# Rows of w_ada loaded one weight chunk ahead of their dot products, with other rates, in a two-layer encoder kernel

## The chip, the cores and the metric

The kernel runs on one core of one Trainium2 chip. The metric is the device time of the whole program in microseconds (us), from runs of the program without a profiler; a trace of one profiled execution stands beside them. On the core, TensorE (PE, with its weight loads as PEld) multiplies matrices, VectorE (DVE), ScalarE (ACT) and GpSimd (POOL) work on elements, and SyncE (SP) issues most of the DMAs. Each engine executes its own instructions in a fixed order; semaphores hold an instruction back until what it reads is there and what it overwrites is no longer needed.

## What is computed

Input is x (512 tokens of 1024 channels) and one conditioning vector c. Two layers, each of three sub-layers on x, each after a norm that is modulated by c:

```python
# mod: for each layer 9 vectors of 1024: silu(c) @ w_ada + b_ada
# (shift, scale, gate) of FFN 1: j = 0, 1, 2; mixer: j = 3, 4, 5; FFN 2: j = 6, 7, 8
h = rms_norm(x, gain) * (1 + scale) + shift
x += 0.5 * gate * ((silu(h @ w_gate) * (h @ w_up)) @ w_down)              # FFN, d_ff = 2816
proj = h @ w_in                                                           # mixer
ya = chunked_relpos_attention(qa, ka, va, ...)
yb = multiscale_pool(ub, w_pool, pool_scale)
yc = forgetting_attention(qc, kc, vc, f, ...)
merged = sum(sigmoid(g_n) * (y_n @ w_branch[n]) for n in (a, b, c))
x += gate * (merged @ w_out)
# then a second FFN with its own shift, scale and gate
```

All is in 32-bit floats. c is known from the start, so the 2 x 9 vectors depend on nothing else that is computed: they have to be there when the norm (shift, scale) or the residual addition (gate) uses them.

## The kernel before

x and the activations lie transposed: 8 blocks of 128 channels, 512 tokens in the free dimension. Every 32-bit operand of a product is split into a high and a low part, and a product is three matmuls (hi·hi, lo·hi, hi·lo: the three lines L119, L120, L121, all in one helper).

**Weights.** `wchunk` (L262) brings a chunk of 512 KB: a DMA on SP's queue into `raw` (L266; 2 buffers), the high part by a cast on ACT into `whi` (L277), the low part by a subtraction on DVE into `wlo` (L279); `whi` and `wlo` have 3 buffers each. A matmul with `wlo` can't begin before that subtraction; the cast can't begin before PE has let go of the buffer. The first thing that `wchunk` does is `side_work`, below.

**Modulation vectors.** Each of the 2 x 9 vectors is 8 blocks of 128, so there are 144 pieces. A piece (`mod_step`, L200) is a DMA of the 128x1024 rows of w_ada (512 KB, on SP's queue, L203) and a dot product with silu(c) on DVE (L206, a multiply with a running sum and a short read of that sum), for a scale also L215 and for a gate L217, on 128x1. 16 of them are done while the program starts, with their own code. The other 128 wait in a queue, in the order layer, j, block, and are taken out by `side_work`: each weight chunk adds MOD_RATE to a credit, and for each whole credit one piece is taken, load and dot together, ahead of the chunk's own load. So on SP a w_ada load stands before a weight load, and on DVE the dot stands before that chunk's subtraction. `mod_need(l, j)` takes out whatever is still missing up to vector j of layer l, at once. It is asked before a norm and before a residual addition.

The rates: 1.0 in the first part of an FFN's gate and up products, 0 in its later parts (which run a 7-product scheme, `seven`), `(1.9, 1.2, 1.5, 1.2)[2 * l + s]` in the down products (FFN s of layer l), 1.0 in the merges of the mixer; none in the attention stages. The rows lie in buffers of the tag "v2" (4 buffers, shared with activations) in the FFNs and of the tag "b" (17 buffers) in the merges.

**Stages.** An FFN runs over d_ff in three parts (6, 8 and 8 blocks of 128 of the 22): gate and up products with the activation, then a down product for the two halves of the output channels (`k_outer`, a weight chunk of 2 blocks of d_ff times 512 channels each; the part of 6 blocks has 2 x 3 chunks). The residual additions are L434 on DVE. The third part takes nothing from the queue once the next sub-layer's norm has been prepared. The mixer does its projections, the attention of branch A and that of branch C with the merge of A between, and then, each as a run of units: four pooling pieces (`pool_front`, with additions on GpSimd, L1033), the merge of C and the merge of B (`merge_units`): for each of 8 blocks d a gate chunk (w_ubg, products with hhi and hlo) and, for every second d, a branch chunk (w_branch) for two d's, then the sum of their products on DVE (L1142) and POOL. After them comes the product with w_out. "Even gates" are those of even d, ahead of which a branch chunk stands.

The order of the work on each engine is that in which the program is written; a table of delayed steps (`later`, `poll`) interleaves the norms and the pooling with the products.

Of the kernel before, what the change touches and what calls it, by code (L numbers as in the profile page):

```python
# [40 lines left out]
def encoder_kernel(tc, xT, c, w_ada, b_ada, gains, w_gate, w_up, w_down, w_qkv, w_f, w_ubg,  # L41
# [22 lines left out]
    def st(shape, dt, tag, bufs):  # L64
        return sb.tile(shape, dt, tag=tag, bufs=bufs, name=nm(tag))
# [4 lines left out]
    def mmt(shape=(P, T)):  # L70
        return ps.tile(list(shape), F32, tag="mm", bufs=4, name=nm("mm"))
# [17 lines left out]
    class Task:  # L89
# [3 lines left out]
        def run(self):  # L93
            fn, self.fn = self.fn, None
            if fn is not None:
                fn()

    def later(delay, fn, group=None):
        t = Task(pe[0] + delay, fn, group)
        tasks.append(t)  # L100
        return t
# [85 lines left out]
    @contextlib.contextmanager  # L187
    def after(what):

        if what in last:  # L190
            with tc.issue_after(last[what]):
                yield
        else:
            yield
# [5 lines left out]
    def mod_step(l, j, d, tag="raw"):  # L200
        raw = st([P, D], F32, tag, {"v2": 4, "raw": NRAW, "b": NB}[tag])
        with after("dma"):
            nc.sync.dma_start(raw, w_ada[l, j, d])  # L203
        m = modc[:, l, j, d:d + 1]
        with after("norm"):
            dot = nc.vector.tensor_tensor_reduce(out=raw, in0=raw, in1=silc[0], scale=1.0,  # L206
                                                 scalar=badac[:, l, j, d:d + 1], op0=ALU.mult, op1=ALU.add,
                                                 accum_out=m).ins
        s, kind = divmod(j, 3)
        if kind == 1:  # L210
            g = gainc[:, l, s, d:d + 1]
            if in_start[0]:
                nc.scalar.activation(apre[:, l, s, d:d + 1], m, AF.Identity, scale=g, bias=g)
                return dot
            return nc.vector.scalar_tensor_tensor(apre[:, l, s, d:d + 1], m, 1.0, g, op0=ALU.add, op1=ALU.mult).ins  # L215
        if kind == 2:
            nc.vector.tensor_scalar(m, m, 0.5, None, op0=ALU.mult)  # L217

    mod_queue = [(l, j, d) for l in range(L) for j in range(9) for d in range(KD)][16:]
    mod_ptr = [0]  # L220
    in_start = [True]
    mod_credit = [0.0]

    mod_tag = ["v2"]

    def mod_pop():
        if mod_ptr[0] < len(mod_queue):
            mod_step(*mod_queue[mod_ptr[0]], mod_tag[0])
            mod_ptr[0] += 1

    def mod_need(l, j):
        while mod_ptr[0] < min(len(mod_queue), (l * 9 + j + 1) * 8 - 16):
            mod_pop()

    MOD_RATE = [1.0]
    in_ffn = [True]
# [12 lines left out]
            yield  # L249

    def side_work(side=True):
        if quiet[0] > 0:
            quiet[0] -= 1
            if quiet[0] == 0:
                gate.clear()
        elif side and in_ffn[0] and mod_tag[0] != "raw":
            mod_credit[0] += MOD_RATE[0]
            while mod_credit[0] >= 1.0:
                mod_credit[0] -= 1.0
                mod_pop()  # L260
# [41 lines left out]
    def xd(d):  # L302
        return x_blocks[d // 2][:, d % 2, :]
# [249 lines left out]
    def apply(parts, func, **kw):  # L553

        o = t1(T)
        n = T // len(parts)
        for i, p in enumerate(parts):
            nc.scalar.activation(o[:, i * n:(i + 1) * n], p, func, **kw)
        return o


    class Ffn:
# [7 lines left out]
        def prefetch(self, xtag):  # L570
            mod_need(self.l, 3 * self.ms + 1)
            self.norm = Norm(self.l, self.ms, xtag)
# [22 lines left out]
        def run(self, nxt):  # L595
            l, s, ms = self.l, self.s, self.ms
            in_ffn[0] = True
            mod_tag[0] = "v2"
            parts = ((0, 6), (6, 8), (14, 8))
            for part, (f0, nf) in enumerate(parts):  # L600
                acts = []
                n = 0
                if part == 0 and self.norm is None:
                    acts = self.start()
                    n = 3
                    blocks = Blocks()
                elif part == 0:
                    g0, u0, g1 = self.pre
                    pg, pu, pg1 = mmt(), mmt(), mmt()
                    for hs in range(2):  # L610
                        self.norm.back(hs, acc if hs else mmt)
                        cols = slice(hs * HALF, (hs + 1) * HALF)
                        if hs == 0:
                            later(FRONT1, lambda: self.norm.front(1, acc))
                            later(BACK1, lambda: self.norm.back(1, acc))
                        for k in range(KD):
                            self.unit(pg, g0, cols, (k,))
                            self.unit(pu, u0, cols, (k,))
                        self.unit(pg1, g1, cols)
                    u1 = self.gate_up(1, 1)  # L620
                    acts.append(self.act(0, pg, pu))
                    pu1 = mmt()
                    self.unit(pu1, u1)
                    acts.append(self.act(1, pg1, pu1))
                    n = 2
                    blocks = Blocks(self.norm.xa, modc[:, l, 3 * ms])
                if part == 0:
                    blocks.schedule(T_FIRST, T_STEP)
                elif part == 1:
                    blocks.finish()  # L630
                MOD_RATE[0] = 0.0 if part else 1.0
                while part and n < nf:
                    both = [apply(p, AF.Silu)
                            for p in seven([w_gate[l, s, f0 + n + i] for i in range(2)], blocks, acc)]
                    ups = seven([w_up[l, s, f0 + n + i] for i in range(2)], blocks, mmt)
                    for i, sg in enumerate(both):
                        acts.append(self.act(n + i, None, ups[i], sg))
                    n += 2
                while n < nf:
                    g = self.gate_up(0, f0 + n)  # L640
                    u = self.gate_up(1, f0 + n)
                    pg, pu = mmt(), mmt()
                    self.unit(pg, g)
                    self.unit(pu, u)
                    acts.append(self.act(n, pg, pu))
                    n += 1
                mod_need(l, 3 * ms + 2)
                MOD_RATE[0] = (1.9, 1.2, 1.5, 1.2)[2 * l + s]
                for c0 in (0, T):
                    def src(c):  # L650
                        r0 = (f0 + 2 * c) * P
                        return w_down[l, s, r0:r0 + 2 * P, c0:c0 + T].rearrange("(k p) c -> p k c", p=P)

                    def ops(hi, lo, kt, j):
                        return (hi[:, j * P:(j + 1) * P], lo[:, j * P:(j + 1) * P],
                                acts[kt][:, 0, :], acts[kt][:, 1, :])

                    last = part == len(parts) - 1
                    if last and c0 == 0 and nxt is not None:
                        nxt.prefetch("v2")  # L660
                        mod_tag[0] = "raw"
                    split = last and c0 > 0
                    hook = None
                    if split:
                        hook = nxt.prefetch_weights if nxt is not None else (lambda: None)
                    for j, hs, o in k_outer(src, nf // 2, ops, hook):
                        d = c0 // P + j
                        residual_tail(d, hs, o, modc[:, l, 3 * ms + 2, d:d + 1], nxt if last else None)
                        if last and nxt is None:
                            cols = slice(0, T) if hs is None else slice(hs * HALF, (hs + 1) * HALF)  # L670
                            nc.sync.dma_start(out[:, d, cols], xd(d)[:, cols])
# [420 lines left out]
    def drain(*gens):  # L1092
        for it in gens:
            for _ in it:
                pass

    class Mixer:
# [1 line left out]
            self.l = l  # L1099

        def prefetch(self, xtag):
            mod_need(self.l, 5)
            self.norm = Norm(self.l, 1, xtag)

        def prefetch_weights(self):
# [2 lines left out]
        def run(self, nxt):  # L1108
            l = self.l
# [56 lines left out]
            for gi in range(4):  # L1166
                b = pool_front(l, gi)
                later(60, lambda gi=gi, b=b: pool_back(l, gi, b, wp, yb))
            in_ffn[0], mod_tag[0], MOD_RATE[0] = True, "b", 1.0
            drain(mc)  # L1170
            poll(True)
            mb = merge_units(l, 1, yb, put_b)
# [8 lines left out]
            for c0 in (0, T):  # L1181
# [8 lines left out]
                for j, hs, o in k_outer(src, 4, ops, nxt.prefetch_weights if c0 else None):  # L1190
                    d = c0 // P + j
# [70 lines left out]
```

## Time and profile before

| | |
|---|---|
| median of 3 runs | 2403.73 us (2403.13 to 2406.02) |
| the profiled execution | 2404.73 us |
| its span, first to last instruction | 2403.0 us, clock 1.00 |
| PE busy | 2359.9 us, 98% |
| DVE busy | 1725.9 us, 72% |
| ACT busy | 1198.4 us, 50% |
| POOL busy | 351.7 us, 15% |
| loads of w_ada | 96 into "v2", 48 into "b", 512 KB each |

A row of a timeline gives start, duration (both us), engine, source line, operation, output <- input by the program's names, shape, and in brackets how long the engine had been idle before it and what it then waited for. Durations of matmuls overlap, since they are pipelined; their starts tell what one costs.

### The profile page before, as it was taken

How to read it: one execution, taken by the hardware profiler on the slowest of the kernel's cores; microseconds unless marked ns; L12 is line 12 of the kernel's file. 1: busy time of each engine (PE TensorE's matmuls, PEld its weight loads, DVE VectorE, ACT ScalarE, POOL GpSimd, SP SyncE). 2: the span in 40 equal slices, each digit the busy share in tenths (PEclk: the TensorE clock that was granted, in tenths of full speed). 3: DMA queues.
4: the chain of work that ended last, by engine and by line, in shares of the span. 5: the costliest groups of instructions: out<-in, count | busy, mean ns of one | idle time of the engine just before them, and what ended most of it. 6: DMA issues, size and time to landing. Idle time of an engine off the chain costs nothing. (4 is left out here: it accounts for less than half of the span.)

```text
span 2403.0 us, 36815 instructions
## 1 busy us (share of the span) xinstructions
PE 2359.9 (98%) x14106; PEld 2085.6 (87%) x14106; DVE 1725.9 (72%) x3070; ACT 1198.4 (50%) x2090; POOL 351.7 (15%) x423
## 2 busy tenths in 40 slices
PE   7999999999999999999999999999999999999999
PEld 5799998778878898989998989978787788989898
DVE  8988866787665476878677878577866655658583
ACT  5353555786632353535553626466865324536252
POOL 3000011144432210000100000102444322000000
PEclk9999999999999999999999999999999999999999
DMA  7736342323345424353325353423233554223322
GB/s 274 238 113 228 99 152 84 93 79 109 108 171 201 175 98 166 105 186 105 132 83 196 104 197 106 141 79 98 80 116 108 193 182 169 71 97 106 101 96 103
DMA packets 116438, 320.94 MB, mean 134 GB/s; under 512 B 11139, under 2 KB 13315, under 8 KB 116261
## 3 DMA queue, kind: packets, MB, share of 16 engines
q1 hardware_dynamic: 115106, 314.38, 38.7%
q0 software_dynamic: 1152, 4.19, 0.4%
q8 instruction: 111, 1.82, 0.3%
q14 instruction: 67, 0.54, 0.1%
q10 hardware_dynamic: 2, 0.00, 0.0%
HBM read 312.16 MB, written 6.38 MB: 133 GB/s over the span
## 5 line engine op out<-in xcount | busy, mean ns | idle before, releaser
L277 ACT CAST whi<-raw 128x1024 fp32r<-128x1024 f32 (+1 forms) x267 | 277.4, 1043 | 431.5 <-PE acc L120 217.9
L279 DVE TENSOR_TENSOR wlo<-raw,whi 128x1024 fp32r<-128x1024 f32 x259 | 319.4, 1237 | 162.2 <-ACT whi L277 159.0
L119 PE MATMUL acc<-b,whi 128*128 128x512 f32 (+1 forms) x960 | 360.7, 376 | 0.2 <-DVE xv L434 0.2
L121 PE MATMUL acc<-b,wlo 128*128 128x512 f32 (+1 forms) x960 | 356.7, 372 | 1.8 <-DVE wlo L279 1.8
L120 PE MATMUL acc<-b,whi 128*128 128x512 f32 (+1 forms) x960 | 357.1, 372 | 0.0
L121 PEld LDWEIGHTS acc<-b,wlo 128*128 128x128 f32 x960 | 180.8, 188 | 34.0 <-DVE wlo L279 2.6
L119 PEld LDWEIGHTS acc<-b,whi 128*128 128x128 f32 x960 | 180.8, 188 | 31.8 <-DVE xv L434 0.6
L120 PEld LDWEIGHTS acc<-b,whi 128*128 128x128 f32 x960 | 181.0, 189 | 29.8
L119 PE MATMUL acc<-hhi,whi 128*128 128x512 f32 x480 | 191.3, 400 | 6.8 <-DVE b L1051 3.1
L121 PE MATMUL acc<-hhi,wlo 128*128 128x512 f32 x480 | 188.1, 393 | 1.0 <-DVE wlo L279 1.0
L120 PE MATMUL acc<-hlo,whi 128*128 128x512 f32 x480 | 188.6, 393 | 0.2 <-DVE hlo L711 0.2
L384 ACT CAST ptb<-v 128x1024 fp32r<-128x1024 f32 x128 | 134.0, 1050 | 97.7 <-DVE v L452 56.2
L385 DVE TENSOR_TENSOR ptb<-v,ptb 128x1024 fp32r<-128x1024 f32 x128 | 156.3, 1223 | 33.8 <-ACT ptb L384 32.3
L384 ACT CAST whi<-raw 128x1024 fp32r<-128x1024 f32 (+1 forms) x128 | 106.7, 834 | 92.1 <-PE acc L120 41.9
L119 PE MATMUL acc<-whi,hhi 128*128 128x512 f32 x336 | 137.8, 411 | 0.9 <-DVE xv L385 0.9
L206 DVE CUSTOM_DVE_ANT_0 v<-v,b,badac 128x1024 f32<-128x1024 f32 x96 | 127.1, 1333 | 15.0 <-DMA v<-in_w_ada_dram 14.8
L121 PE MATMUL acc<-whi,hlo 128*128 128x512 f32 x336 | 131.9, 393 | 0.0
L120 PE MATMUL acc<-wlo,hhi 128*128 128x512 f32 x336 | 131.6, 392 | 0.0
L385 DVE TENSOR_TENSOR wlo<-raw,whi 128x1024 fp32r<-128x1024 f32 (+1 forms) x128 | 121.6, 950 | 6.5 <-ACT whi L384 5.0
L434 DVE SCALAR_TENSOR_TENSOR xv<-acc,modc,xv 128x512 f32<-128x512 f32 (+1 forms) x112 | 77.3, 690 | 62.2 <-PE acc L121 62.0
L119 PEld LDWEIGHTS acc<-hhi,whi 128*128 128x128 f32 x480 | 90.6, 189 | 25.6 <-DVE b L1051 4.0
L329 POOL TENSOR_TENSOR ssum<-ssum,t 128x256 f32<-128x256 f32 (+1 forms) x45 | 46.5, 1034 | 442.8 <-ACT t L328 442.7
(315 smaller groups left out, 6667.5 us busy)
## 6 DMA issues: line engine op xcount, KB each, us to landing
v<-in_w_ada_dram SPq DMA_DIRECT2D x96, 512.0 KB, 5.3
raw<-in_w_down_dram SPq DMA_DIRECT2D x88, 512.0 KB, 3.7
raw<-in_w_up_dram SPq DMA_DIRECT2D x82, 512.0 KB, 4.0
raw<-in_w_gate_dram SPq DMA_DIRECT2D x79, 512.0 KB, 3.7
raw<-in_w_ubg_dram SPq DMA_DIRECT2D x56, 512.0 KB, 3.6
b<-in_w_ada_dram SPq DMA_DIRECT2D x48, 512.0 KB, 4.6
raw<-in_w_qkv_dram SPq DMA_DIRECT2D x42, 512.0 KB, 3.9
raw<-in_w_branch_dram SPq DMA_DIRECT2D x24, 512.0 KB, 3.7
```

Of the source, the lines that this page charges most:

```text
L119: mm(o, lh, rh, start=start, stop=False)
L120: mm(o, lh, rl, start=False, stop=False)
L121: mm(o, ll, rh, start=False, stop=stop)
L206: dot = nc.vector.tensor_tensor_reduce(out=raw, in0=raw, in1=silc[0], scale=1.0, scalar=badac[:, l, j, d:d + 1], op0=ALU.mult, op1=ALU.add ...
L277: nc.scalar.copy(hi, raw)
L279: lo_eng.tensor_tensor(lo, raw, hi.bitcast(F32), op=ALU.subtract)
L329: nc.gpsimd.tensor_tensor(self.ssum[:, cols], self.ssum[:, cols], q, op=ALU.add)
L384: nc.scalar.copy(hi, src)
L385: nc.vector.tensor_tensor(lo, src, hi.bitcast(F32), op=ALU.subtract)
L434: nc.vector.scalar_tensor_tensor(x, acc_j, gate, x, op0=ALU.mult, op1=ALU.add)
```

## The change

Outside the start of the program, taking a piece from the queue now issues the load only. The dot is kept in a list, and is written out at the beginning of the next chunk's `side_work` (`mod_flush`), or when a further piece is taken out within the same chunk (then all but the last one kept are written out). `mod_need` keeps up to two loads ahead while it takes several, and writes out the dots up to what it was asked for. Beside that, the mixer's norm asks for vectors up to j = 4 in place of 5 (the gate of the mixer is asked for before the w_out product, as it was before), the rate in all down products is 1.2, and that in the merges 1.2.

```diff
@@ mod_step
         with after("dma"):
             nc.sync.dma_start(raw, w_ada[l, j, d])
+        dot = lambda: mod_dot(raw, l, j, d)
+        return dot() if in_start[0] else dot
+
+    def mod_dot(raw, l, j, d):
         m = modc[:, l, j, d:d + 1]
...
-    def mod_pop():
+    loaded = []
+
+    def mod_pop(behind=1):
+        mod_flush(behind)
         if mod_ptr[0] < len(mod_queue):
-            mod_step(*mod_queue[mod_ptr[0]], mod_tag[0])
+            loaded.append(mod_step(*mod_queue[mod_ptr[0]], mod_tag[0]))
             mod_ptr[0] += 1
 
+    def mod_due(l, j):
+        return min(len(mod_queue), (l * 9 + j + 1) * 8 - 16)
+
+    def mod_flush(behind=0):
+        while len(loaded) > behind:
+            loaded.pop(0)()
+
     def mod_need(l, j):
-        while mod_ptr[0] < min(len(mod_queue), (l * 9 + j + 1) * 8 - 16):
-            mod_pop()
+        while mod_ptr[0] < mod_due(l, j):
+            mod_pop(2)
+        while mod_ptr[0] - len(loaded) < mod_due(l, j):
+            loaded.pop(0)()
...
     def side_work(side=True):
+        mod_flush()
         if quiet[0] > 0:
...
-                MOD_RATE[0] = (1.9, 1.2, 1.5, 1.2)[2 * l + s]
+                MOD_RATE[0] = 1.2
...
-            mod_need(self.l, 5)
+            mod_need(self.l, 4)
...
-            in_ffn[0], mod_tag[0], MOD_RATE[0] = True, "b", 1.0
+            in_ffn[0], mod_tag[0], MOD_RATE[0] = True, "b", 1.2
```

The number of loads taken in each stage, counted on SP:

| stage | before | after |
|---|---|---|
| layer 0, FFN 1, first down product | 13 | 9 |
| layer 0, FFN 1, second down product | 15 | 9 |
| layer 0, merges and w_out | 24 | 29 |
| layer 0, FFN 2 | 21 | 21 |
| layer 1, FFN 1 | 25 | 23 |
| layer 1, merges and w_out | 24 | 28 |
| layer 1, FFN 2, first part | 0 | 3 |

The other 22 loads, the same number in both, are in the time before the first down product. Two places show the order. The first is VectorE at the end of layer 0's first down product; `wlo` are splits of weight chunks, L206 (L210 after) dots, L434 (L451) residual additions. Before:

```order
L434 SCALAR_TENSOR_TENSOR xv_85<-acc_756,modc,xv_85 128x512
L206 ISA v_180_923,modc<-v_180_923,b_73,badac 128x1024
L206 ISA modc 128x1
L279 TENSOR_TENSOR wlo_930<-raw_927,whi_929 128x1024
L215 SCALAR_TENSOR_TENSOR apre<-modc,gainc 128x1
L206 ISA v_184_933,modc<-v_184_933,b_73,badac 128x1024
L206 ISA modc 128x1
L206 ISA v_185_937,modc<-v_185_937,b_73,badac 128x1024
L206 ISA modc 128x1
L215 SCALAR_TENSOR_TENSOR apre<-modc,gainc 128x1
L279 TENSOR_TENSOR wlo_944<-raw_941,whi_943 128x1024
```

And after, at the same two splits:

```order
L210 ISA v_176_911,modc<-v_176_911,b_73,badac 128x1024
L210 ISA modc 128x1
L451 SCALAR_TENSOR_TENSOR xv_78<-acc_754,modc,xv_78 128x512
L210 ISA v_180_920,modc<-v_180_920,b_73,badac 128x1024
L210 ISA modc 128x1
L210 ISA v_181_922,modc<-v_181_922,b_73,badac 128x1024
L210 ISA modc 128x1
L451 SCALAR_TENSOR_TENSOR xv_85<-acc_755,modc,xv_85 128x512
L296 TENSOR_TENSOR wlo_916<-raw_913,whi_915 128x1024
L451 SCALAR_TENSOR_TENSOR xv_85<-acc_756,modc,xv_85 128x512
L296 TENSOR_TENSOR wlo_927<-raw_924,whi_926 128x1024
```

Between the last two splits stood two dots, and stands one residual addition.

The second place is layer 1's merge of branch C, from a branch chunk's split to that of the gate of d = 4. VectorE before:

```order
L279 TENSOR_TENSOR wlo_19713<-raw_19710,whi_19712 128x1024
L206 ISA b_19716,modc<-b_19716,b_19248,badac 128x1024
L206 ISA modc 128x1
L1142 SCALAR_TENSOR_TENSOR t_3695_19652<-t_3693_19637,acc_19639 128x512
L206 ISA b_19768,modc<-b_19768,b_19248,badac 128x1024
L206 ISA modc 128x1
L215 SCALAR_TENSOR_TENSOR apre<-modc,gainc 128x1
L206 ISA b_19821,modc<-b_19821,b_19248,badac 128x1024
L206 ISA modc 128x1
L279 TENSOR_TENSOR wlo_19722<-raw_19719,whi_19721 128x1024
```

VectorE after:

```order
L1159 SCALAR_TENSOR_TENSOR t_3689_19629<-t_3687_19614,acc_19616 128x512
L296 TENSOR_TENSOR wlo_19694<-raw_19691,whi_19693 128x1024
L210 ISA b_19698,modc<-b_19698,b_19220,badac 128x1024
L210 ISA modc 128x1
L210 ISA b_19750,modc<-b_19750,b_19220,badac 128x1024
L210 ISA modc 128x1
L296 TENSOR_TENSOR wlo_19703<-raw_19700,whi_19702 128x1024
```

Between the two splits stood three dots, and stand two. SyncE's issues there, before (`raw` from w_branch and w_ubg are weight chunks, `b` from w_ada rows):

```order
L266 DMA raw_19710<-in_w_branch_dram 128x2x512
L203 DMA b_19716<-in_w_ada_dram 128x1024
L266 DMA raw_19719<-in_w_ubg_dram 128x1024
L203 DMA b_19768<-in_w_ada_dram 128x1024
L266 DMA raw_19772<-in_w_ubg_dram 128x1024
L203 DMA b_19821<-in_w_ada_dram 128x1024
```

And after:

```order
L283 DMA raw_19691<-in_w_branch_dram 128x2x512
L203 DMA b_19698<-in_w_ada_dram 128x1024
L283 DMA raw_19700<-in_w_ubg_dram 128x1024
L203 DMA b_19750<-in_w_ada_dram 128x1024
L283 DMA raw_19752<-in_w_ubg_dram 128x1024
L203 DMA b_19802<-in_w_ada_dram 128x1024
```

The last row of w_ada that stands ahead of the gate's split (b_19821 before, b_19750 now) was issued behind the load of the chunk after that gate's (raw_19772), and is now issued ahead of it (raw_19752).

## The prediction

> **What bounds the kernel now.** I read the busy table of the page first, then a table of stages, then the TensorE rows that start late, then what stands on VectorE ahead of each of them.
>
> ```profile
> span 2403.0 us, 36815 instructions
> PE 2359.9 (98%) x14106; PEld 2085.6 (87%) x14106; DVE 1725.9 (72%) x3070; ACT 1198.4 (50%) x2090; POOL 351.7 (15%) x423
> ```
>
> TensorE (PE) is the bound: 43.1 us of the span without a matmul is all that any other engine can give back while the matmuls stay the same, and the change leaves the matmuls alone. By stages (columns: us, then busy time of PE, PEld, DVE, ACT, POOL, clock, DMA share, GB/s):
>
> ```profile
> 0.00:60.00 60.00, 44.51 (x161) 32.55 (x162) 50.81 (x79) 34.60 (x54) 18.40 (x16) 1.00 0.76 274
> 60.00:120.00 60.00, 58.01 (x253) 46.98 (x254) 56.11 (x86) 19.18 (x22) 0.00 (x0) 1.00 0.74 238
> 120.00:385.00 265.00, 264.79 (x1900) 250.24 (x1898) 211.79 (x347) 132.41 (x219) 16.36 (x22) 1.00 0.41 142
> 385.00:685.00 300.00, 292.50 (x1505) 240.63 (x1504) 212.34 (x516) 199.32 (x422) 98.94 (x146) 1.00 0.32 100
> 685.00:830.00 145.00, 143.43 (x632) 118.35 (x631) 87.08 (x122) 43.40 (x56) 37.76 (x22) 1.00 0.52 189
> 1200.00:1560.00 360.00, 359.16 (x2425) 333.31 (x2425) 273.80 (x451) 170.87 (x277) 13.36 (x16) 1.00 0.41 137
> 1560.00:1868.00 308.00, 299.19 (x1542) 245.88 (x1541) 218.63 (x540) 203.16 (x434) 105.43 (x156) 1.00 0.31 97
> 1868.00:2015.00 147.00, 144.48 (x636) 118.88 (x635) 88.56 (x126) 43.72 (x56) 37.39 (x26) 1.00 0.53 194
> ```
>
> PE idles 15.5 us in the first 60 us, whose orders of work on VectorE, ScalarE and SyncE the change leaves alone for most of it, and 7.5 and 8.8 us in the two attention stages, which have no w_ada dot products. What the change can reach is 2.0 us at 60 to 120 (layer 0, the first down product), 0.2 and 0.8 us in the other FFN stages shown, 1.6 and 2.5 us in the two merges. These are the late matmuls in the three stages that matter:
>
> ```profile
> 112.94 0.50 PE L119 MATMUL acc<-b,whi 128*128 128x512 f32 x1 [0.18 <-DVE xv L434]
> 115.27 0.50 PE L121 MATMUL acc<-b,wlo 128*128 128x512 f32 x1 [0.23 <-DVE wlo L279]
> 118.96 0.50 PE L121 MATMUL acc<-b,wlo 128*128 128x512 f32 x1 [1.58 <-DVE wlo L279]
> 694.33 0.50 PE L119 MATMUL acc<-hhi,whi 128*128 128x512 f32 x1 [1.57 <-DVE b L1051]
> 1905.58 0.39 PE L119 MATMUL acc<-hhi,whi 128*128 128x512 f32 x1
> 1905.81 0.39 PE L120 MATMUL acc<-hlo,whi 128*128 128x512 f32 x1
> 1907.15 0.50 PE L121 MATMUL acc<-hhi,wlo 128*128 128x512 f32 x1 [0.95 <-DVE wlo L279]
> ```
>
> A matmul of 512 columns starts 0.23 us after the one ahead (1905.58 to 1905.81). The late one starts 1.34 us after it, so the loss is 1.11 us, 0.16 more than the wait in brackets. I add that 0.16 to each wait.
>
> **The change, part by part.**
>
> First, fewer dots in layer 0's first down product (13 loads become 9). VectorE and, for the last two weight chunks, the ScalarE casts that precede the splits:
>
> ```profile
> 110.93 1.28 DVE L206 CUSTOM_DVE_ANT_0 v<-v,b,badac 128x1024 f32<-128x1024 f32 x1
> 112.80 1.27 DVE L206 CUSTOM_DVE_ANT_0 v<-v,b,badac 128x1024 f32<-128x1024 f32 x1
> 114.00 1.22 DVE L279 TENSOR_TENSOR wlo<-raw,whi 128x1024 fp32r<-128x1024 f32 x1
> 115.21 1.28 DVE L206 CUSTOM_DVE_ANT_0 v<-v,b,badac 128x1024 f32<-128x1024 f32 x1
> 116.41 1.28 DVE L206 CUSTOM_DVE_ANT_0 v<-v,b,badac 128x1024 f32<-128x1024 f32 x1
> 117.69 1.22 DVE L279 TENSOR_TENSOR wlo<-raw,whi 128x1024 fp32r<-128x1024 f32 x1
> ```
>
> ```profile
> 107.17 1.05 ACT L277 CAST whi<-raw 128x1024 fp32r<-128x1024 f32 x1 [1.93 <-PE acc L120]
> 111.01 1.05 ACT L277 CAST whi<-raw 128x1024 fp32r<-128x1024 f32 x1 [2.79 <-DMA raw<-in_w_down_dram]
> ```
>
> whi of the last chunk is there at 112.06, its wlo only at 118.91, because dots stand between. Each costs VectorE 1.2 us from start to start (115.21 to 116.41). In the new order the last two splits have only a residual row between them and no dot, and four dots fewer have run before: 4 x 1.2 = 4.8 us. The last split then starts 4.8 us earlier or more, against losses of 0.34, 0.39 and 1.74 us (0.18, 0.23 and 1.58, each with 0.16). All three go: **−2.5 us**. It can't be much more, since the stage's whole PE idle time is 2.0 us by busy time. At worst it is 0, if the raw chunk is late: that last cast waited 2.79 us for its DMA. It landed by 111.01, and PE wanted wlo from about 117.2 (118.96 less 1.74); I take the full gain. Dots that move to later stages are priced there.
>
> Second, the loads ahead. Where a dot product waits for its row, what is queued behind it waits too:
>
> ```profile
> DVE b L206 <- DMA b<-in_w_ada_dram: 35.6, 21, 3.9
> DVE v L206 <- DMA v<-in_w_ada_dram: 14.8, 17, 1.9
> ```
>
> That is 50.4 us in 38 waits of VectorE, but VectorE is not the bound; only a wait that makes a split late counts. The one that does, in layer 1's merge (VectorE's two rows, ScalarE's, SyncE's issue of the load):
>
> ```profile
> 1904.67 1.28 DVE L206 CUSTOM_DVE_ANT_0 b<-b,b,badac 128x1024 f32<-128x1024 f32 x1 [2.47 <-DMA b<-in_w_ada_dram]
> 1905.88 1.22 DVE L279 TENSOR_TENSOR wlo<-raw,whi 128x1024 fp32r<-128x1024 f32 x1
> ```
>
> ```profile
> 1902.84 1.05 ACT L277 CAST whi<-raw 128x1024 fp32r<-128x1024 f32 x1 [6.35 <-PE acc L120]
> ```
>
> ```profile
> 1894.50 1.21 SPq L203 DMA_DIRECT2D b<-in_w_ada_dram  x1
> ...
> 1898.20 0.38 SPq L203 DMA_DIRECT2D b<-in_w_ada_dram  x1
> ```
>
> The row took 6.4 us from issue to use. In the new order the dot ahead of this split is of a row issued one chunk earlier on SyncE, here the place of the row at 1894.50, 3.7 us before, so it has landed when VectorE comes to it. The split then starts after its cast, at 1903.9, 2.0 us earlier: **−1.1 us**. The other 37 waits end in no late matmul, so removing them is worth 0. SyncE issues the same 144 rows; each goes out just ahead of a weight chunk instead of just behind one, so a weight load may be pushed back by the time of one load. The raw buffers are asked for more than a chunk ahead, so I take 0. Bounds: nothing, and the 2.79 us of the late w_down chunk above, once.
>
> Third, the rest of the rates. Layer 0's second down product goes from 15 to 9 loads and layer 1's from 12 to 10, where PE idles 0.2 and 0.8 us in all: 0 for fewer dots. In exchange the merges with their output product get 5 dots more in layer 0 and 4 in layer 1 (6.0 and 4.8 us of VectorE, which is free for 57.9 and 58.4 us there), and layer 1's FFN2 gets 3. What hides them is the slack of the splits. The tightest are those of the even gates (2, 4, 6 in the first merge, 0, 2, 4, 6 in the second, 7 a layer), where the cast has to wait for a buffer that PE frees:
>
> ```profile
> 732.30 1.28 DVE L206 CUSTOM_DVE_ANT_0 b<-b,b,badac 128x1024 f32<-128x1024 f32 x1 [3.06 <-DMA b<-in_w_ada_dram]
> 734.31 1.23 DVE L279 TENSOR_TENSOR wlo<-raw,whi 128x1024 fp32r<-128x1024 f32 x1 [0.52 <-ACT whi L277]
> ```
>
> ```profile
> 736.43 0.39 PE L121 MATMUL acc<-hhi,wlo 128*128 128x512 f32 x1
> ```
>
> wlo is done at 735.54 and used at 736.43, 0.89 us spare, and VectorE stood 0.52 us before it: a dot there may end 1.4 us later than now. One dot more is 1.2 us and is preceded by a wait of 3.06 us that the earlier load takes away. So 0; bounds 0 and 14 places x 1.2 = 17 us.
>
> Fourth, asking for shift and scale only: in both versions the counter is already past what is asked for when the norm asks, so nothing moves by it: 0 (by it alone at most one dot, 1.2 us, either way).
>
> The stall at 694.33 and its like in layer 1 stay: the two dots ahead of it stand in the same VectorE rows as before.
>
> Sum: 2404.73 − 2.5 − 1.1 = 2401.1 on the profiled execution, which is 1.0 us above the median of the runs; against that median of 2403.73 the forecast is **2400.1 us**, 0.15% less. A measurement of this kernel can tell about 0.2% (4.8 us) from no change, so this counts as the same, near the edge.
>
> **A rule against it.** VectorE and GpSimd slow each other where they overlap:
>
> ```profile
> 681.61 1.04 POOL L1033 TENSOR_TENSOR strip<-strip 128x512 f32<-128x512 f32 x1
> 687.43 1.90 POOL L1033 TENSOR_TENSOR strip<-strip 128x512 f32<-128x512 f32 x1
> ```
>
> ```profile
> 688.36 2.05 DVE L206 CUSTOM_DVE_ANT_0 b<-b,b,badac 128x1024 f32<-128x1024 f32 x1
> ```
>
> A dot of 1.28 us took 2.05, an addition of 1.04 us took 1.90. [...] By that rule each of the 9 further dots of the merges that meets an addition ahead of an even gate's split costs 0.6 us (2.0 against 1.4 spare): at most 5.4 us, and the sum would be 2405.5; by the slack alone it stays 2400.1.
>
> **Rivals.**
> (S, slower) The merges' further dots reach the even gates' splits. A place with one dot more, slowed by an overlapping GpSimd addition as at 688.36, holds the split 1.2 + 0.8 = 2.0 us longer, 0.6 more than the 1.4 spare. Speaking for it: 0.53 of the DMA time is taken there, so rows can be late again. Against it: the waits of 3.06 and 2.47 us go. Slower by over 0.2% needs 4.8 + 3.6 = 8.4 us, 0.6 at each of 14 places; with 0.8 each it is 2400.1 + 11 = 2411.
> (N, does not do what it says) The rows land late even so, or dots still hold the splits: four dots still precede the second-last split of the first down product. Gains then between 0 and 1.1: 2402.6 to 2403.7.
> (G, more gain) The stall at 694.33 (1.57 + 0.16) and its like go as well, since the two dots, whose rows are loaded earlier, may finish before GpSimd's additions begin: 2 x 1.73 = 3.5 more, 2396.6. For it: the additions are slowed by the dots alone. Against it: those dots did not wait for their rows now.
>
> **How the numbers follow.** The forecast 0.42, G and like gains 0.24, N 0.18, S 0.16. Within the forecast's own spread of about 2 us (2398 to 2402) some 0.14 of its 0.42 falls under 2398.9, the limit of faster; with 0.22 of G that makes faster 0.36. Slower than 2408.5 takes S alone: 0.16. The rest is 0.48. The range reaches to G's 2396.6 less 0.6 below, and above past N to half of S's smaller costs: 2396 to 2407.
>
> **What the profile after would show.** At 110 to 119 the L121 rows in the usual step of 0.23 us, and the PE busy of 60 to 120 at 59.5 or more. In the waits, the 35.6 and 14.8 us in front of the dots fallen to under 10 together. The windows of the merges with VectorE's time about 6 and 5 us higher, PE's idle time 1.6 and about 1.4 us. S would show L121 rows of gates in the merges waiting for wlo; N would show a wlo row still late at about 118. I am wrong if PE idles elsewhere: in the first 60 us, where a w_ada row now goes out ahead of a weight chunk, or in layer 0's first down product waiting for raw.

## The result, and the profile after

| | before | after |
|---|---|---|
| median, 22 runs each | 2403.87 us | 2400.09 us (2398.17 to 2403.12) |
| ratio, 95% interval | | 0.9986 (0.998 to 0.9992) |
| span of the profiled execution | 2403.0 us | 2398.8 us |

The time fell by 3.8 us, 0.14%. Both places that the prediction named are clean. TensorE's waits by what they wait for (us in total, times, longest) had three waits of matmuls for a split (`wlo`) before, shown here, and after has none:

```profile
PE acc L121 <- DVE wlo L279: 2.8, 3, 1.6
```

The stages of after (us, then busy time of PE, PEld, DVE, ACT, POOL, clock, DMA share, GB/s):

```profile
60.00:120.00 60.00, 59.92 (x256) 49.32 (x257) 54.10 (x79) 19.18 (x23) 0.00 (x0) 0.97 0.64 211
685.00:830.00 145.00, 143.37 (x632) 118.29 (x631) 92.65 (x137) 42.84 (x54) 40.43 (x22) 1.00 0.56 204
1868.00:2015.00 147.00, 145.37 (x641) 119.83 (x640) 95.31 (x136) 44.57 (x57) 38.58 (x22) 1.00 0.56 204
```

PE idles 0.08 us in the first down product (2.0 before), as much as before in layer 0's merge and 0.9 us less in layer 1's. VectorE has 5.6 and 6.8 us more to do in the merges, and it makes nothing late.

At the end of the first down product the two splits now stand 1.8 us apart, with one residual row between:

```profile
110.24 1.22 DVE L296 TENSOR_TENSOR wlo<-raw,whi 128x1024 fp32r<-128x1024 f32 x1
111.38 0.74 DVE L451 SCALAR_TENSOR_TENSOR xv<-acc,modc,xv 128x512 f32<-128x512 f32 x1
112.04 1.22 DVE L296 TENSOR_TENSOR wlo<-raw,whi 128x1024 fp32r<-128x1024 f32 x1
```

In layer 1's merge the split that had stood behind a dot with a wait of 2.47 us follows its cast, with idle time ahead of it:

```profile
1900.15 1.27 DVE L210 CUSTOM_DVE_ANT_0 b<-b,b,badac 128x1024 f32<-128x1024 f32 x1
1901.35 0.08 DVE L210 DVE_READ_ACCUMULATOR2_ANT modc<- 128x1 f32 x1
1902.21 1.23 DVE L296 TENSOR_TENSOR wlo<-raw,whi 128x1024 fp32r<-128x1024 f32 x1 [0.78 <-ACT whi L294]
```

Start to start, the late matmuls at these two places cost 2.47 and 1.12 us before and nothing now. Two things in the trace were not forecast. Five matmuls of the 7-product scheme, at 157, at 1454 and 1465 and at 2332 and 2343 us, waited for ScalarE before and do not now, together 2.5 us; three of them, as they stood in the trace of before:

```profile
156.82 0.39 PE L128 MATMUL acc<-b,whi 128*128 128x256 f32 x1 [0.21 <-ACT v L546]
...
1454.01 0.39 PE L128 MATMUL mm<-b,whi 128*128 128x256 f32 x1 [0.41 <-ACT v L546]
...
2332.39 0.38 PE L128 MATMUL mm<-b,whi 128*128 128x256 f32 x1 [0.29 <-ACT v L546]
```

Against that, the clock fell for a few us in this execution of after:

```profile
60.00:65.00 5.00, 4.92 (x14) 3.80 (x15) 5.00 (x8) 1.49 (x3) 0.00 (x0) 0.66 0.72 238
```

At a mean clock of 0.66 over 5 us, 1.7 us of work is lost by estimate (5 x 0.34); the matmuls from 61.40 to 64.39 us start 0.43 us apart, where those of before start 0.23 us apart at the same place. Sum of the traces: −2.5 − 1.1 − 2.5 + 1.7 = −4.4, against −4.2 between the spans.

### The profile page after: what moved, and what is told of

Its sections match the earlier page's. It is cut to its first block, busy times and chain, and to the rows that moved or that the text cites. A ratio compares the mean times of both kernels' runs of the same rounds, so it can differ in the third digit from the quotient of the medians.

```text
span 2398.8 us, 36815 instructions
## 1 busy us (share of the span) xinstructions
PE 2359.2 (98%) x14106; PEld 2086.4 (87%) x14106; DVE 1729.7 (72%) x3070; ACT 1199.3 (50%) x2090; POOL 357.2 (15%) x423
## 5 line engine op out<-in xcount | busy, mean ns | idle before, releaser
L121 PE MATMUL acc<-b,wlo 128*128 128x512 f32 (+1 forms) x960 | 356.6, 371 | 0.0
L121 PEld LDWEIGHTS acc<-b,wlo 128*128 128x128 f32 x960 | 180.8, 188 | 31.4
L121 PE MATMUL acc<-hhi,wlo 128*128 128x512 f32 x480 | 187.9, 392 | 0.0
L121 PE MATMUL acc<-whi,hlo 128*128 128x512 f32 x336 | 132.0, 393 | 0.0
L210 DVE CUSTOM_DVE_ANT_0 v<-v,b,badac 128x1024 f32<-128x1024 f32 x87 | 115.7, 1340 | 16.7 <-DMA v<-in_w_ada_dram 16.6
L451 DVE SCALAR_TENSOR_TENSOR xv<-acc,modc,xv 128x512 f32<-128x512 f32 (+1 forms) x112 | 77.4, 691 | 63.9 <-PE acc L121 63.9
```

The source lines that it names most:

```text
L121: mm(o, ll, rh, start=False, stop=stop)
L451: nc.vector.scalar_tensor_tensor(x, acc_j, gate, x, op0=ALU.mult, op1=ALU.add)
```

## The experiments

All ratios are to the kernel before, run on the same chip in the same session; intervals are 95%.

| run | what it is | ratio (interval) |
|---|---|---|
| rates | before, with 1.2 in down products and merges | 1.0004 (0.9995 to 1.0013) |
| ahead | loads ahead alone | 0.9984 (0.9975 to 0.9993) |
| need5 | after, norm asks for vector 5 | 1.0003 (0.9994 to 1.0012) |
| rates4 | after without the loads ahead | 1.0001 (0.9992 to 1.001) |
| after2 | after again | 0.9988 (0.9979 to 0.9997) |
| twoahead | after, dots in the merges two chunks behind | 0.9981 (0.9973 to 0.999) |
| merge2 | after, rate 2.0 in the merges | 1.0016 (1.0008 to 1.0025) |
| poolfree | after, no dots beside the last pooling piece | 0.9971 (0.9961 to 0.9982) |
| aheadpool | ahead, the same | 0.9978 (0.9969 to 0.9987) |
| evengate | after, credit given by kind of chunk | 0.9974 (0.9964 to 0.9985) |
| rates4pool | rates4, no dots beside the last pooling piece | 0.9976 (0.9966 to 0.9986) |

### The parts apart

**rates.** The numbers without the rest.

```diff
-                MOD_RATE[0] = (1.9, 1.2, 1.5, 1.2)[2 * l + s]
+                MOD_RATE[0] = 1.2
...
-            in_ffn[0], mod_tag[0], MOD_RATE[0] = True, "b", 1.0
+            in_ffn[0], mod_tag[0], MOD_RATE[0] = True, "b", 1.2
```

> The kernel before with 1.2 in all down products and in the merges; load and dot together as before, and the mixer's norm asks for the gate too. Theory: what ended the three late matmuls of layer 0's first down product is the four dots fewer, so they go here too (-2.5 us), while the late split in layer 1's merge comes from a row loaded too late and stays, or moves to another even gate (0): 2401.4 us against 2403.9 of before. Rival (the loads ahead are what gains): no change, 2403.9.

Median 2406.0 us against 2404.75: no gain. Yet the first down product had no late matmul in this trace, as the theory said, nor had layer 1's merge a late split. The gain was given back at two places that the theory had not seen: matmuls 2.5 us late at 342 to 345 (0.69, 1.06 and 0.70), in layer 0's third down product, and one 3.2 us late at 697, behind the last pooling piece (1.7 before):

```profile
341.54 0.50 PE L121 MATMUL acc<-b,wlo 128*128 128x512 f32 x1 [0.53 <-DVE wlo L279]
343.62 0.50 PE L119 MATMUL acc<-b,whi 128*128 128x512 f32 x1 [0.89 <-ACT whi L277]
344.88 0.50 PE L121 MATMUL acc<-b,wlo 128*128 128x512 f32 x1 [0.53 <-DVE wlo L279]
...
697.07 0.50 PE L119 MATMUL acc<-hhi,whi 128*128 128x512 f32 x1 [3.06 <-ACT t L1083]
```

Around the last of them the clock was lower, 0.92 and 0.91 on the means of 690 to 700 and 700 to 710 us, another 1.7 us by estimate (0.8 + 0.9).

**ahead.** The change with the old numbers back in place.

```diff
-                MOD_RATE[0] = 1.2
+                MOD_RATE[0] = (1.9, 1.2, 1.5, 1.2)[2 * l + s]
...
-            mod_need(self.l, 4)
+            mod_need(self.l, 5)
...
-            in_ffn[0], mod_tag[0], MOD_RATE[0] = True, "b", 1.2
+            in_ffn[0], mod_tag[0], MOD_RATE[0] = True, "b", 1.0
```

> The changed kernel with the old rates (1.9, 1.2, 1.5, 1.2 and 1.0) and the norm asking for the gate: the loads ahead alone. Theory: the late split of layer 1's merge goes (-1.1 us); in the first down product all dots stay, one of the two ahead of the last split now stands ahead of it and one of the others behind the split, so of the 2.5 us about 1.2 goes: 2401.6 us. Rival (the loads ahead are what gains): both places free of late matmuls, 2400.1. Second rival (the rates do all): 2403.9.

2401.14 us against 2404.75, ratio 0.9984, as much as the whole change, and both places are free of late matmuls: the first rival's case. VectorE at the last two splits of the first down product, with all the old dots:

```profile
110.82 1.22 DVE L296 TENSOR_TENSOR wlo<-raw,whi 128x1024 fp32r<-128x1024 f32 x1
111.95 1.28 DVE L210 CUSTOM_DVE_ANT_0 v<-v,b,badac 128x1024 f32<-128x1024 f32 x1
113.15 0.08 DVE L210 DVE_READ_ACCUMULATOR2_ANT modc<- 128x1 f32 x1
113.15 1.22 DVE L296 TENSOR_TENSOR wlo<-raw,whi 128x1024 fp32r<-128x1024 f32 x1
```

One dot stands between the splits where two stood. The first of them comes 3.2 us earlier (110.82, 114.00 before), the last one 4.5 (113.15, 117.69 before). So the loads ahead take these stalls away by the order in which dots and splits stand, with as many dots as before.

**need5.** The edit that the prediction priced at nothing, undone.

```diff
-            mod_need(self.l, 4)
+            mod_need(self.l, 5)
```

> The changed kernel, the mixer's norm asking for vector 5 again. Theory from the run with the rates alone: at the lower rates 24 rows are taken by the time that norm is prepared, 24 is what vector 4 needs and 32 what vector 5 needs, so 8 rows are loaded at once, in layer 0, between two weight loads of the third down product; that run lost 2.5 us there. Here too: late matmuls at about 340, 2 to 3 us over the changed kernel. Rival (the edit costs nothing, as the prediction had it; two loads ahead hide it): no late matmul there, the changed kernel's time.

2403.45 us: all the gain is gone. SyncE's issues at the place, and two of the four late matmuls (1.14 and 0.69 us late from start to start; two more, 0.30 and 0.92, follow at 364 and 365):

```profile
319.63 13.73 SPq L203 DMA_DIRECT2D v<-in_w_ada_dram  x8
333.41 1.87 SPq L283 DMA_DIRECT2D raw<-in_w_down_dram  x2
```

```profile
342.34 0.50 PE L119 MATMUL acc<-b,whi 128*128 128x512 f32 x1 [0.97 <-ACT whi L294]
343.60 0.50 PE L121 MATMUL acc<-b,wlo 128*128 128x512 f32 x1 [0.53 <-DVE wlo L296]
```

Eight rows are asked for at once, for a tag of 4 buffers; their issues take SyncE 13.7 us, and the weights of the down product stand behind them in its queue and go out from 333.41 us on. At the new rates exactly 24 of the queue's rows are taken when this norm asks; vector 4 needs 24, vector 5 needs 32.

**rates4.** All the new numbers, load and dot together: the run rates with one edit more.

```diff
-            mod_need(self.l, 5)
+            mod_need(self.l, 4)
```

> The kernel before with all the numbers of the change (1.2 everywhere, the norm asking for vector 4), load and dot together: the changed kernel without the loads ahead. Theory: as the run with the rates alone, without its loss of 2.5 us at 342 to 345; layer 0's first down product free of late matmuls (-2.5), and, with a third dot beside the last pooling piece of layer 0, its late matmul 3.2 us late in place of 1.7 (+1.5): 2.5 us under that run, some 1 to 2 us under the kernel before. Rival (the loads ahead are needed for any gain): the time before. Second rival (the numbers do all): 3.6 us under before.

2403.85 us against 2403.32, the first rival's figure. The loss at 342 to 345 is gone, the first down product is clean, and still there is no gain. What is left is the place behind the last pooling piece. VectorE and PE there:

```profile
691.55 0.17 DVE L1040 TENSOR_TENSOR ssum<-hd,b 128x16 f32<-128x16 f32 x1
691.64 0.21 DVE L217 TENSOR_SCALAR modc<-modc 128x1 f32<-128x1 f32 x2
691.76 1.28 DVE L206 CUSTOM_DVE_ANT_0 b<-b,b,badac 128x1024 f32<-128x1024 f32 x1
692.96 0.08 DVE L206 DVE_READ_ACCUMULATOR2_ANT modc<- 128x1 f32 x1
692.96 0.69 DVE L385 TENSOR_TENSOR ptb<-ssum,ptb 128x512 fp32r<-128x512 f32 x1
```

```profile
693.92 0.80 PE L119 MATMUL acc<-hhi,whi 128*128 128x512 f32 x1 [3.04 <-ACT t L1083]
```

```profile
690.00:700.00 10.00, 6.96 (x19) 5.20 (x18) 7.24 (x16) 2.64 (x4) 3.09 (x2) 0.66 0.29 116
```

A third dot got between the pooling piece and what PE waits for, the wait grew to 3.04 us, and behind it the clock was lower: 0.66 on the mean of these 10 us, another 2.4 us late by the matmuls' starts (0.86 over 25 us for 685 to 710). The late matmul, what the clock took and four L128 matmuls waiting for ScalarE (1.8 us) are what separates it from after in the traces.

### The place behind the last pooling piece

**poolfree.** The changed kernel without dots in the first chunks of the merge.

```diff
             in_ffn[0], mod_tag[0], MOD_RATE[0] = True, "b", 1.2
+            mod_credit[0] = -2.4
             drain(mc)
```

> The changed kernel with the credit of the merges set to -2.4 at their begin, so that no dot runs while the last pooling piece is added up on GpSimd. Theory: the additions of that piece took 1.9 us in place of 1.04 because two dots ran beside them, so the late matmul behind them (1.80 us in each layer) goes: 3.6 us less than the changed kernel, 2396.5. Rival: the chain ScalarE, GpSimd, VectorE is too long without them too, and the matmul stays over 1 us late: 2399 to 2400.

2397.6 us against 2404.75, ratio 0.9971 where the changed kernel has 0.9986: the theory's figure. GpSimd's second and third addition of that piece, with dots beside them in the changed kernel:

```profile
686.52 1.90 POOL L1050 TENSOR_TENSOR strip<-strip 128x512 f32<-128x512 f32 x1
...
688.54 1.86 POOL L1050 TENSOR_TENSOR strip<-strip 128x512 f32<-128x512 f32 x1
```

And undisturbed, in poolfree:

```profile
685.45 1.04 POOL L1050 TENSOR_TENSOR strip<-strip 128x512 f32<-128x512 f32 x1
686.55 0.11 POOL L1049 MEMSET strip<- 128x16 f32 x1
686.61 1.04 POOL L1050 TENSOR_TENSOR strip<-strip 128x512 f32<-128x512 f32 x1
```

Nothing is late behind the piece in either layer (1.80 us each in after). A new late split stands at an even gate, 0.87 us from start to start:

```profile
733.45 0.50 PE L121 MATMUL acc<-hhi,wlo 128*128 128x512 f32 x1 [0.71 <-DVE wlo L296]
```

**rates4pool.** The same edit on rates4.

> The run rates4 (all the numbers of the change, load and dot together) with the credit of -2.4 at the begin of the merges. In rates4 one dot more than in the changed kernel stood between the last pooling piece and its split; the matmul behind was 3.2 us late (1.8 in the changed kernel) and the clock fell to 0.84 to 0.89 behind it. Theory (that place is all that the loads ahead are worth beside the new numbers): the place is free of late matmuls, 5 to 7 us under rates4 and as good as poolfree, 2397 to 2398. Rival (the loads ahead are worth something elsewhere too): 2399 or more, with late splits in the merges or in the FFN stages.

2398.08 us against 2403.46, ratio 0.9976 where rates4 has 1.0001, 6 us more. The theory holds: with that place free, the new numbers without loads ahead come out as good as with them, within the intervals. Its trace has one split 0.68 us late at 733, as poolfree has, and four L128 matmuls late by 2.1 us in all.

**aheadpool.** Loads ahead, old numbers, the same edit.

> Loads ahead, the old rates and the norm asking for vector 5, and no dots beside the last pooling piece (credit of -2.4 at the begin of the merges). Theory: the loads ahead alone take both late places away, the credit the two behind the pooling, and at a rate of 1.0 no chunk of the merges has two dots, so the late split at 733 of the run poolfree (0.87 us) is not there either: 7 us under the kernel before, 0.5 to 1 us better than poolfree. Rival: the higher rates of the down products cost something that the lower ones save: as poolfree or worse.

2398.76 us, ratio 0.9978. The stalls behind the pooling are gone, but the gain over "ahead" is small, and the 0.5 to 1 us over poolfree did not come: a split 1.50 us late at an even gate of layer 1 (1902 us) is new, and VectorE waits 39.0 us for rows in the merges (27.0 in after). The new late split is of the kind that the loads ahead were to remove: the dot ahead of it still waits 3.04 us for its row. VectorE's two rows and PE's:

```profile
1899.31 1.28 DVE L210 CUSTOM_DVE_ANT_0 b<-b,b,badac 128x1024 f32<-128x1024 f32 x1 [3.04 <-DMA b<-in_w_ada_dram]
...
1900.52 1.22 DVE L296 TENSOR_TENSOR wlo<-raw,whi 128x1024 fp32r<-128x1024 f32 x1
```

```profile
1901.80 0.50 PE L121 MATMUL acc<-hhi,wlo 128*128 128x512 f32 x1 [1.33 <-DVE wlo L296]
```

### The dots of the merges

**merge2.** Rate 2.0.

```diff
-            in_ffn[0], mod_tag[0], MOD_RATE[0] = True, "b", 1.2
+            in_ffn[0], mod_tag[0], MOD_RATE[0] = True, "b", 2.0
```

> The changed kernel with a rate of 2.0 in the merges, two dots for each weight chunk. Theory (1.4 us spare at the even gates, more elsewhere): one dot more of 1.2 us fits, no late split in layer 0's merges, within 1 us of the changed kernel, 2399 to 2401. Rival S (the dots reach the splits, 0.6 us or more at each even gate of layer 0 and at some of layer 1): L121 waits for wlo at 7 to 14 places, 2404 to 2411.

2409.12 us against 2404.75, ratio 1.0016. "One dot more fits" fell. Four splits come late and a cast at a fifth place, in place of the 7 to 14 that S wanted; the four splits:

```profile
703.57 0.50 PE L121 MATMUL acc<-hhi,wlo 128*128 128x512 f32 x1 [1.56 <-DVE wlo L296]
...
723.47 0.50 PE L121 MATMUL acc<-hhi,wlo 128*128 128x512 f32 x1 [1.61 <-DVE wlo L296]
...
1893.83 0.50 PE L121 MATMUL acc<-hhi,wlo 128*128 128x512 f32 x1 [1.57 <-DVE wlo L296]
...
1910.76 0.50 PE L121 MATMUL acc<-hhi,wlo 128*128 128x512 f32 x1 [0.32 <-DVE wlo L296]
```

What makes them late is only in part VectorE's time: the rows are also in the way of the weights. SyncE issues seven rows in a run, 4.55 us from 699.71 us on, ahead of a branch chunk, and the casts at 702.24, 715.35 and 722.98 us wait 2.01, 5.77 and 2.83 us for their raw chunk. The DMA share of layer 0's merge is 0.71 at 264 GB/s (0.56 and 204 in after).

**twoahead.** The dots of the merges held back one chunk more.

```diff
     def side_work(side=True):
-        mod_flush()
+        mod_flush(1 if mod_tag[0] == "b" else 0)
...
-                mod_pop()
+                mod_pop(2 if mod_tag[0] == "b" else 1)
```

> The changed kernel, in the merges each dot written out two weight chunks behind its load in place of one. Theory (VectorE's waits for w_ada rows cost nothing where no split is late): the 27.0 us of waits for rows in the merges fall below 10, the time stays that of the changed kernel within 1 us, the stalls at 693 and 1879 stay or grow with one dot more or fewer in front. Rival (VectorE's waits for the rows are part of the path): the time falls with them, by 2 us or more.

2399.78 us, ratio 0.9981, not told apart from after. But the waits did not fall, so the run doesn't test what it was made for:

```profile
DVE b L210 <- DMA b<-in_w_ada_dram: 29.0, 19, 3.8
DVE v L210 <- DMA v<-in_w_ada_dram: 14.6, 18, 1.6
```

In the compiled order the dots stand nearly where they stood in after, though the program writes each of them a chunk later: in layer 0's merges one dot alone stands behind a split that it stood ahead of, and in layer 1's the order of dots and splits is the same. So the words ahead of the prediction that each engine's order is that in which the program is written don't hold for these dots: the order seems to be set anew when the program is built, and the compiled order has to be read to know where a dot stands. With the same order, one split of layer 1's merge still made a matmul 0.85 us late here, at 1936 us: the dot ahead of it waited 1.63 us for its row, and 0.78 us in after, where nothing is late.

**evengate.** The credit given by kind of chunk.

```diff
             if d % 2 == 0:
+                MOD_RATE[0] = 0.0
                 wb[0] = wchunk(w_branch[l, n, d:d + 2].rearrange("a p k c -> p a k c"), (2, 4, P))
+            MOD_RATE[0] = 0.0 if n == 2 and d == 0 else 2.0
             gh, gl = wchunk(w_ubg[l, 4 + n * KD + d], (KD, P))
```

> The changed kernel with the credit of the merges given by chunk: none ahead of a branch chunk (its dots would stand ahead of an even gate's split), two ahead of each gate chunk, none in the first pair of branch C (beside the last pooling piece). Theory (the even gates are where splits come late, and the pooling piece is the other loss): no L121 late for a split in the merges and nothing late behind the pooling, about 3.6 us under the changed kernel and 0.9 under the run poolfree, 7.5 us under the kernel before. Rival (two dots for a gate chunk reach the next split): late matmuls at odd gates or behind branch chunks, 0.5 us or more each.

2397.36 us against 2403.32, ratio 0.9974. PE has no idle time left in either merge:

```profile
685.00:830.00 145.00, 145.00 (x640) 119.80 (x639) 94.90 (x140) 43.27 (x56) 36.51 (x21) 1.00 0.62 224
1868.00:2015.00 147.00, 147.00 (x648) 121.37 (x647) 94.91 (x140) 44.41 (x57) 37.84 (x22) 1.00 0.63 226
```

It takes 30 rows in each layer's merges and w_out product (29 and 28 in the changed kernel, 48 and 14 in merge2), two at a time as merge2 does, and none of their dots makes a matmul of the merges late. It is no faster than poolfree within the intervals. These two, 6 to 7 us under the kernel before, are 2.5 to 3 us faster than the changed kernel by their medians.

### The two kernels once more

**after2.**

> The changed kernel once more, beside the next ones: about 3.7 us under the kernel before. Theory: the late matmuls of its first trace return at the same places (1.8 us late at about 693 and 1879, none waiting for a split). The gain of some 2 us that stood at the 7-product scheme (five L128 matmuls late by 0.3 to 0.6 us in the trace of before, none in that of the changed kernel) either returns, then the change makes it, or comes and goes with the execution.

2399.2 us against 2403.31. The late matmul behind the pooling returns in both layers at 1.78 us, the places in the first down product and the merges are free again, no L128 matmul is over 0.3 us late, and the clock is whole at 60 to 65 us.

**before2.**

> The kernel before once more, for its trace. Theory: the three late matmuls of the first down product and the late split in layer 1's merge return within 0.1 us, being set by the order. Open: whether the L128 matmuls that waited for ScalarE in the 7-product scheme (five, 2.5 us, some waits for gate weights behind them) come back at the same places.

2404.99 us in a single run. The first down product's three late matmuls return, the first of them 1.28 us late in place of 0.34, the other two at 0.37 and 1.74; the split in layer 1's merge is 0.55 us late in place of 1.12. In these two traces, then, the same matmuls are late, and by how much differs: 3.9 us in this execution, 3.6 in the other. Late L128 matmuls return at 2333 and 2343 us and another appears at 1137; those at 157, 1454 and 1465 do not. Over all traces, those at about 2324 to 2346 stand as a pair in before, before2, rates, ahead, evengate and rates4pool, one alone in aheadpool, merge2 and need5, and none in after, after2, poolfree, twoahead and rates4. They wait for a copy on ScalarE; why it is late in some kernels was not found, so the 2.5 us that they are worth between the traces of before and after is without a known cause.

## Why the prediction was right, and where it was not

**The sum.** 2400.1 forecast, 2400.09 measured. The two terms, −2.5 and −1.1, were read from start-to-start times and came as read: 2.47 and 1.12 us in the traces. That the sum also fits to the last digit is luck: a further −2.5 (L128) and +1.7 (clock) in the profiled execution were not in it, and the terms themselves differ by 0.3 us in sum between the two traces of before.

**First term, its reason.** "Four dots fewer" is one way to the clean first down product (rates, rates4), but not the needed one: ahead has all the old dots and is clean too, where I had expected 1.2 of the 2.5 us. The two parts of the change cure the same splits, so their gains don't add.

**Second term.** Right in the change as a whole. The reason, a row issued one chunk earlier, is not proved: rates and rates4, without loads ahead, have no late split there either, since the new counts put other dots at that gate. And aheadpool, with loads ahead, has a dot that waits 3.04 us for its row ahead of a late split: a dot written a chunk behind its load does not by itself find its row there.

**The third part, the rates at nothing.** Right for the change: 5.6 and 6.8 us more of VectorE's time in the merges were hidden, as were the dots in layer 1's FFN 2. The slack "a dot may end 1.4 us later" is not to be trusted for more: merge2 lost there, partly by way of the weight loads, which I had taken at 0.

**The fourth part, wrong.** I wrote that the counter is past what is asked in both versions, so that nothing moves, at most one dot or 1.2 us. In the changed kernel it stands at 24, exactly what vector 4 needs, and vector 5 would need 32. Without this edit the change loses its whole gain: 0.9988 against 1.0003 in one session, 3.6 us. The edit is what pays for the lower rates. I priced it against the kernel before, where it does change nothing; it had to be priced beside the other edits.

**The waits for rows, wrong.** 35.6 and 14.8 us were to fall under 10 together; they are 27.0 and 16.6:

```profile
DVE b L210 <- DMA b<-in_w_ada_dram: 27.0, 18, 3.0
DVE v L210 <- DMA v<-in_w_ada_dram: 16.6, 20, 2.3
```

I had each row go out just ahead of a weight chunk instead of just behind one. But SyncE holds the raw loads until a buffer is free (in after they waited 857.0 us in all for the splits that read one, 182 times), and the row still goes out just behind one: at 726.93, 7.8 us before the next raw load at 734.72 in the merge, where before it went out at 727.78, 7.8 us before the raw load at 735.56. VectorE, with little else to do, is there before it lands. That the time fell while 43.6 of 50.4 us of waits stayed shows what the prediction did say: nearly all of those waits are not on the path. merge2 shows it from the other side: 1.7 us of waits for rows are left in its merges, and it is the slowest run.

**The rivals.** S did not come at 1.2 and came at 2.0, at fewer places. Of N, the rows did land late even so, at no cost to PE in after; that dots still hold the splits is wrong by the rows at 110.24 and 112.04. G was rightly left out: the two dots stood beside the pooling piece as before, and the late matmul stayed (1.74 to 1.80 us). Its price, 3.5 us, is right: poolfree gains 3.6 us over the changed kernel by the ratios ((0.9986 − 0.9971) x 2404; the intervals overlap by 0.0002).

**The rule against the change.** VectorE and GpSimd slowed each other at the place where it mattered. Beside the last pooling piece of after two dots took 2.06 and 2.05 us, where one takes 1.28 undisturbed, and the additions at 686.52 and 688.54 took 1.90 and 1.86 us; with the dots away, in poolfree, these additions took 1.04, and 3.6 us of PE's time came back. In the rows of the prediction the dot and the addition ran side by side as well, and took 0.77 and 0.86 us longer. Not every overlap costs that: the addition ahead of these two, at 684.91 us in after, has a dot beside it from 685.46 us on and takes 1.53 us, as in poolfree without one. The sum of 2405.5 did not come. No run shows the 0.6 us for each further dot from which I worked it out: no split of a gate came late in the merges of after, and the four late splits of merge2 held L121 for 0.32 to 1.61 us.

## What to carry to other kernels

Read what a bound engine loses from its own late starts, stage by stage, and price a change only by those; here 43.6 us of another engine's waits stayed at no cost that the traces show. Price edits in the order in which they enable one another: the lower rate and the smaller demand are one edit, and with the lower rate but not the smaller demand (rates, need5) the gain was gone. And where side work slows a chain that the bound engine waits for, move it to where nothing waits: a line that holds it off two weight chunks was worth as much as the whole change.

## What was not expected of the hardware

In four of the fourteen traces TensorE's clock was lower for a few microseconds behind waits of PE, and it cost 1.7 or 2.4 us, beside waits of 1.24 to 3.06 us. In after it was 0.53, 0.50, 0.50 and 0.76 in the slices of 1 us from 61 to 65 us and 1.00 in those on both sides: 1.7 us by estimate (0.47 + 0.50 + 0.50 + 0.24), behind a wait of 1.24 us. Behind the wait of 3.04 us at 694 us in rates4 it was 0.66 on the mean of 10 us, and 2.4 us were lost by the matmuls' starts; in rates, with one of 3.06 us at the same place, it was 0.92 and 0.91 for two spans of 10 us. None of the waits of 1.6 or 1.7 us at that place had it. After the wait at 58 to 60 us the clock stood at 0.66 for 60 to 65 us in two traces (after and need5), and whole in the twelve others, with the same wait (1.24 us in before and in after), so the fall doesn't follow from the length of one wait alone. What decides whether a wait is followed by such a dip, and what ends the dip, no run here shows.

The mean clock of each whole run shows how often it was lower. It was 1.0 in all 93 runs of the kernel before that stand beside the experiments, and 0.998 or 0.999 in 4 of the 22 runs of after and 1 of 11 of after2, but in 9 of 11 of rates, 10 of 11 of rates4, 10 of 11 of merge2 and 6 of 11 of need5; in the rest it was lower in none to 3 of 7. In rates, the two runs at 1.0 took 2402.5 and 2403.0 us, the nine others 2406.6 us on the mean; in need5 the two means are 2403.5 and 2404.3. So a part of what such variants lose is the clock and not the wait itself; these runs are too few to say how large a part.
